# One-hot tables made by two wide VectorE instructions, and gate-table evictions with the token as innermost index

## The chip, the cores and the metric

The kernel runs on one core of a Trainium2 chip. TensorE multiplies matrices, VectorE and ScalarE work elementwise, GpSimd (POOL) does a little elementwise work, and each of them, with SyncE (SP), can issue DMAs. The metric is the time of one execution in microseconds on the device.

## What is computed

Two transformer blocks follow one another on 256 tokens of width 1024. The first mixes tokens by an mLSTM and by differential attention and then applies `peer`, a layer of 16384 one-neuron experts; the second has sparse attention, a convolution and a feed-forward layer. The change lies in `peer`:

```python
def block(xb):                                    # 128 tokens
    q = (xb @ w_query).reshape(TOKEN_BLOCK, P_HEADS, 2, P_HALF)
    s = jnp.einsum('thpk,hpnk->thpn', q, sub_keys).astype(jnp.float32)
    sv, si = lax.top_k(s, P_TOPK)                 # 16 best of 128, for each half
    cand = sv[:, :, 0, :, None] + sv[:, :, 1, None, :]
    cidx = si[:, :, 0, :, None] * N_KEYS + si[:, :, 1, None, :]
    fv, fpos = lax.top_k(cand, P_TOPK)            # (last two axes flattened)
    eidx = jnp.take_along_axis(cidx, fpos, axis=-1)
    g = jax.nn.softmax(fv, axis=-1)
    u = u_tab[eidx]
    act = jax.nn.gelu(jnp.einsum('td,thkd->thk', xb, u), approximate=False)
    return jnp.einsum('thk,thkd->td', (g * act), v_tab[eidx])
```

So each token has 8 heads x 16 = 128 picked experts, each with a gate `g`. An expert's number is (first key) x 128 + (second key).

## The kernel before

The kernel gathers nothing. It computes the activations of all 128 blocks of 128 experts for all 256 tokens, and multiplies them by a gate table that is zero for experts that were not picked. For one block `b`, the unit `U(b)` loads a weight block of `peer_u`, splits it into a high and a low part (`whi`, a ScalarE cast at line 112; `wlo`, a VectorE subtraction at line 120), and `chunk` runs 8 x 3 matmuls of 128x256 (lines 163 to 165). ScalarE applies the gelu (line 793) and writes `act[b]`. Units are converted four to five ahead of their use (`fill`), and loads, of two units each, run in three buffers (`wraw`) on SP's queue.

The gate table is built in the loop at lines 947 to 965, in 32 groups of 8 tokens (`OG`). The 128 partitions are a token's 128 picks. `ib[:, 0]` and `ib[:, 1]` hold the first and the second key of each pick, `gp[:, 0]` and `gp[:, 1]` the gate as a high and a low part, `iob` the numbers 0 to 127 in f16. For each token `onehots` writes with VectorE `o`, a one-hot row of the second key (line 941), and `go`, the one-hot row of the first key times the gate, once for each part (line 943): 24 instructions of 128 elements for a group. TensorE multiplies `o` (stationary) by both parts of `go` (line 958), which gives a 128x128 matrix for the token: 16 matmuls for a group, four tokens to a PSUM bank. ScalarE copies a bank, scaled, to `stg` (line 961), with the tokens `TG` = 16 elements to a row there; after two groups a DMA on ScalarE's queue writes `stg` to the table `gd` in DRAM (line 963). Behind each group stands one unit `U`.

The order is the order of the code on each engine. In a group: `onehots` of the next group, the matmuls and evictions of this one, every second time the DMA, then the unit with its `whi`, `wlo`, matmuls and gelu. `o` and `go` have two buffers, the two PSUM tiles of `side()` and the two of `main()` likewise.

After the loop seven units remain; then the expert loop (lines 1015 to 1023) multiplies each `act` by its part of the table, reread from DRAM as `gt` (line 979), splits the product into `wh` and `wl` (lines 996 and 1001) and accumulates it with `peer_v` into four PSUM banks.

Of the kernel before, what the change touches and what calls it, by code (L numbers as in the profile page):

```python
# [13 lines left out]
F32 = mybir.dt.float32  # L14
F32R = mybir.dt.float32r
BF = mybir.dt.bfloat16
F16 = mybir.dt.float16
# [3 lines left out]
OP = mybir.AluOpType  # L21
# [4 lines left out]
T = 256  # L26
# [9 lines left out]
UKEEP = 7  # L36
TG = 16
OG = 8
GI = 8
LOADS = 9  # L40
SPLITS = 4
GSCALE = 32768.0
# [22 lines left out]
class Kx:  # L65
# [696 lines left out]
    def peer(self):  # L762
        nc, tc, a = self.nc, self.tc, self.a
# [4 lines left out]
        drp = ctx.enter_context(tc.tile_pool(name="pdr", bufs=1, space=DRAM))  # L768
        c1 = ExitStack()
        pz = c1.enter_context(tc.tile_pool(name="pz", bufs=1))  # L770
        gp = pz.tile([128, 2, T], F32, name="gp")
        ib = pz.tile([128, 2, T], F32, name="ib")
        acts = {}
        c2 = ExitStack()
        pk = c2.enter_context(tc.tile_pool(name="pk", bufs=1))
# [20 lines left out]
        with c2:  # L796
# [39 lines left out]
            for hd in range(1, 8):  # L836
# [5 lines left out]
                for i in range(2 if hd > 1 else 0):  # L842
                    p = self.unit("w_query", 2 * hd + i, h)
# [11 lines left out]
            pf_ = c2.enter_context(tc.tile_pool(name="pf", bufs=1))  # L855
# [4 lines left out]
            def finish():  # L860
                g = [pf_.tile([128, 8, 16], F32, name=f"g{tt}") for tt in range(2)]
                pf = [pf_.tile([128, 2, 8, 16], F32, name=f"pf{tt}") for tt in range(2)]
                sxf = [pf_.tile([128, 2, 8, 16], F32, name=f"sxf{tt}") for tt in range(2)]
                for tt in range(2):
                    v = fv[tt]
                    nc.vector.tensor_tensor(g[tt], v, v[:, :, 0:1].to_broadcast([128, 8, 16]), op=OP.subtract)
                    nc.scalar.activation(g[tt], g[tt], AF.Exp)
                for tt in range(2):
                    pi = pft.tile([128, 2, 8, 16], U32, name="pi")
                    nc.vector.tensor_scalar(pi[:, 0], fx[tt], 4, None, op0=OP.logical_shift_right)  # L870
                    nc.vector.tensor_scalar(pi[:, 1], fx[tt], 15, None, op0=OP.bitwise_and)
                    nc.vector.tensor_copy(sxf[tt].rearrange("p s h a -> p h s a"), sx[tt])
                    nc.vector.tensor_copy(pf[tt], pi)
                for tt in range(2):
                    gz = pft.tile([128, 8], F32, name="gz")
                    nc.vector.tensor_reduce(gz, g[tt], axis=AX.X, op=OP.add)
                    nc.vector.reciprocal(gz, gz)
                    nc.vector.tensor_tensor(g[tt], g[tt], gz[:, :, None].to_broadcast([128, 8, 16]), op=OP.mult)
                for _ in range(FW):
                    yield  # L880
                for tt in range(2):
                    p = self.side()
                    for j, src in enumerate((sxf[tt][:, 0], sxf[tt][:, 1], pf[tt][:, 0], pf[tt][:, 1])):
                        nc.tensor.transpose(p[:, j * 128:(j + 1) * 128], src.rearrange("p a b -> p (a b)"),
                                            self.ident)
                    ts = slice(tt * 128, (tt + 1) * 128)
                    p = p.rearrange("p (k s t) -> p k s t", k=2, s=2)
                    nc.scalar.copy(sxT[:, :, ts], p[:, 0])
                    nc.scalar.copy(posT[:, :, ts], p[:, 1])
                p = self.side()  # L890
                for tt in range(2):
                    nc.tensor.transpose(p[:, tt * 128:(tt + 1) * 128], g[tt].rearrange("p a b -> p (a b)"),
                                        self.ident)
                slot = pf_.tile([128, T], F32, name="slot")
                nc.scalar.mul(slot, p[:, :T], GSCALE)
                yield
                acc = self.bank(0)
                last = None
                for a0 in range(0, 16, FA):
                    cur = []  # L900
                    for a in range(a0, a0 + FA):
                        pb = self.side()
                        nc.tensor.matmul(pb, pick[:, a].rearrange("p h w -> p (h w)"),
                                         sxT.rearrange("p s t -> p (s t)"), start=True, stop=True)
                        t = pft.tile([128, 2 * T], BF, name="hit", bufs=2 * FA)
                        nc.vector.scalar_tensor_tensor(t, posT.rearrange("p s t -> p (s t)"), float(a), pb,
                                                       op0=OP.is_equal, op1=OP.mult)
                        cur.append((a, t))
                    yield
                    for a, t in cur:  # L910
                        nc.tensor.matmul(acc, identb, t, start=a == 0, stop=a == 15)
                nc.scalar.copy(ib, acc.rearrange("p (j t) -> p j t", j=2))
                g16 = pf_.tile([128, T], F16, name="g16")
                nc.vector.tensor_copy(g16, slot)
                nc.vector.tensor_copy(gp[:, 0], g16)
                nc.vector.tensor_tensor(gp[:, 1], slot, gp[:, 0], op=OP.subtract)

            self.side_cycle = ("s", "s", "a1", "a2")
            self.tasks.append(finish())
            while self.tasks:  # L920
                self.tick()
                if len(pre) > T // OG + UKEEP:
                    U(pre.popleft())
            while len(pre) > T // OG + UKEEP:
                U(pre.popleft())
            self.side_cycle = ("s",)

        with ExitStack() as c3:
            pg = c3.enter_context(tc.tile_pool(name="pg", bufs=1))
            pgt = c3.enter_context(tc.tile_pool(name="pgt", bufs=2))  # L930
            iob = pg.tile([128, 128], F16, name="iob")
            nc.gpsimd.iota(iob, pattern=[[1, 128]], base=0, channel_multiplier=0,
                           allow_small_or_imprecise_dtypes=True)
            stg = None

            def onehots(og):
                o = pgt.tile([128, OG, 128], F16, name="o")
                go = pgt.tile([128, OG, 2, 128], F16, name="go")
                for i in range(OG):
                    t = slice(og * OG + i, og * OG + i + 1)  # L940
                    nc.vector.tensor_scalar(o[:, i], iob, ib[:, 1, t], None, op0=OP.is_equal)  # L941
                    for j in range(2):
                        nc.vector.tensor_scalar(go[:, i, j], iob, ib[:, 0, t], gp[:, j, t],  # L943
                                                op0=OP.is_equal, op1=OP.mult)
                return o, go

            nxt = onehots(0)
            for og in range(T // OG):
                o2, go = nxt
                if og + 1 < T // OG:  # L950
                    nxt = onehots(og + 1)
                if og % (TG // OG) == 0:
                    stg = pgt.tile([128, 128, TG], F32, name="stg")
                for q in range(OG // 4):
                    p = self.side().rearrange("p (t i) -> p t i", t=4)
                    for i in range(4):
                        for j in range(2):
                            nc.tensor.matmul(p[:, i], o2[:, q * 4 + i], go[:, q * 4 + i, j],  # L958
                                             start=i == 0 and j == 0, stop=j == 1, skip_group_check=True)
                    e0 = (og % (TG // OG)) * OG + q * 4  # L960
                    nc.scalar.mul(stg[:, :, e0:e0 + 4].rearrange("p i t -> p t i"), p, 1.0 / GSCALE)
                if og % (TG // OG) == TG // OG - 1:
                    nc.scalar.dma_start(gd[:, og * OG // TG], stg)
                if len(pre) > UKEEP:
                    U(pre.popleft())
# [3 lines left out]
        with ExitStack() as c4:  # L969
# [5 lines left out]
            def gload(i):  # L975
                if i * GI < NB:
                    gts[i] = gt = pv.tile([128, 8 * (T + 2)], F32, name="gt")[:, :8 * T].rearrange(
                        "p (g e) -> p g e", g=T // TG)
                    (nc.gpsimd if i < 2 else nc.scalar).dma_start(gt, gd[:, :, i * GI:(i + 1) * GI].rearrange("p g i t -> p g (i t)"))

            wts = {}

            def w_mult(b):
                if b >= NB:
                    return
                t = acts[b]
                gv = gts[b // GI][:, :, (b % GI) * TG:(b % GI + 1) * TG]
                tv = t.rearrange("p (g t) -> p g t", t=TG)
                nc.vector.tensor_tensor(tv, tv, gv, op=OP.mult)  # L989
                if b % GI == GI - 1:  # L990
                    gload(b // GI + 2)

# [583 lines left out]
```

## Time and profile before

| | us |
|---|---|
| median of 3 runs | 1547.26 (1546.43 to 1547.27) |
| the profiled execution | 1546.58 |
| span of its trace | 1544.9 |
| TensorE busy in the span | 1427.4 (92%) |
| VectorE busy | 1204.3 (78%) |
| ScalarE busy | 765.9 (50%) |
| GpSimd busy | 240.9 (16%) |

A busy time is the union of an engine's instructions. Matmuls overlap one another, so what a matmul costs is read from the start of one to the start of the next; on VectorE and ScalarE too the next instruction can start a little before the last one's end. The granted clock is TensorE's, as a share of full speed.

### The profile page before, as it was taken

How to read it: one execution, taken by the hardware profiler on the slowest of the kernel's cores; microseconds unless marked ns; L12 is line 12 of the kernel's file. 1: busy time of each engine (PE TensorE's matmuls, PEld its weight loads, DVE VectorE, ACT ScalarE, POOL GpSimd, SP SyncE). 2: the span in 40 equal slices, each digit the busy share in tenths (PEclk: the TensorE clock that was granted, in tenths of full speed). 3: DMA queues.
4: the chain of work that ended last, by engine and by line, in shares of the span. 5: the costliest groups of instructions: out<-in, count | busy, mean ns of one | idle time of the engine just before them, and what ended most of it. 6: DMA issues, size and time to landing. Idle time of an engine off the chain costs nothing.

```text
span 1544.9 us, 28187 instructions
## 1 busy us (share of the span) xinstructions
PE 1427.4 (92%) x11206; PEld 1351.2 (87%) x11208; DVE 1204.3 (78%) x2723; ACT 765.9 (50%) x1225; POOL 240.9 (16%) x143
## 2 busy tenths in 40 slices
PE   3897888979998999999999999999989989999997
PEld 2777777978777779999999999999989979989997
DVE  7887789997999996777777776666689968775554
ACT  3445554434555555544444454454564485554443
POOL 1443253310000000000000000000057740310000
PEclk8898989989999999999999999999999999999999
DMA  9365543434444458888888887677534434435642
GB/s 377 141 239 181 191 150 136 154 122 162 161 167 186 169 206 308 297 307 312 303 308 286 294 285 233 219 244 241 179 114 163 164 109 164 164 138 190 205 165 81
DMA packets 106068, 317.36 MB, mean 205 GB/s; under 512 B 5584, under 2 KB 34640, under 8 KB 103632
## 3 DMA queue, kind: packets, MB, share of 16 engines
q1 hardware_dynamic: 65696, 250.54, 45.8%
q10 hardware_dynamic: 39408, 61.87, 11.4%
q0 software_dynamic: 832, 3.15, 0.6%
q8 instruction: 88, 1.44, 0.4%
q14 instruction: 44, 0.36, 0.1%
HBM read 297.71 MB, written 17.83 MB: 204 GB/s over the span
## 4 chain that ended last, share of the span: by engine, by line
PE 56%; DVE 34%; ACT 4%; DMA 3%; issue 2%; POOL 1%; DVEq 0%; SPq 0%; ACTq 0%; POOLq 0%
PE a L163 10%; PE a L164 10%; PE a L165 10%; PE m L163 8%; PE m L164 8%; PE m L165 8%; DVE go L943 7%; DVE wlo L120 5%; DVE a L1138 3%; DVE o L941 3%; DVE junk L326 2%; DMA mraw<-in_ada_w 1%; ACT whi L112 1%; DMA raw<-in_ada_w 1%; DVE mdt L294 1%
## 5 line engine op out<-in xcount | busy, mean ns | idle before, releaser
L163 PE MATMUL m<-hi,whi 128*128 128x256 f32 x1816 | 526.5, 290 | 9.2 <-DVE cacc L556 6.0
L165 PE MATMUL m<-hi,wlo 128*128 128x256 f32 x1816 | 516.9, 285 | 9.4 <-DVE wlo L120 9.4
L164 PE MATMUL m<-lo,whi 128*128 128x256 f32 x1816 | 517.0, 285 | 0.0
L112 ACT CAST whi<-raw 128x1024 fp32r<-128x1024 f32 x428 | 444.6, 1046 | 50.1 <-DMA raw<-in_peer_v 19.5
L120 DVE TENSOR_TENSOR wlo<-raw,whi 128x1024 fp32r<-128x1024 f32 x350 | 437.7, 1269 | 30.9 <-ACT whi L112 23.0
L163 PEld LDWEIGHTS m<-hi,whi 128*128 128x128 f32 x1816 | 352.1, 194 | 16.1 <-issue 5.4
L165 PEld LDWEIGHTS m<-hi,wlo 128*128 128x128 f32 x1816 | 351.1, 193 | 10.7 <-DVE wlo L120 10.4
L164 PEld LDWEIGHTS m<-lo,whi 128*128 128x128 f32 x1816 | 351.7, 194 | 0.6
L165 PE MATMUL a<-wh,wlo 128*128 128x256 f32 x1024 | 288.2, 281 | 0.0
L164 PE MATMUL a<-wl,whi 128*128 128x256 f32 x1024 | 288.2, 281 | 0.0
L163 PE MATMUL a<-wh,whi 128*128 128x256 f32 x1024 | 287.9, 281 | 0.0
L120 POOL TENSOR_TENSOR wlo<-raw,whi 128x1024 fp32r<-128x1024 f32 x81 | 202.2, 2510 | 223.0 <-ACT whi L112 196.1
L165 PEld LDWEIGHTS a<-wh,wlo 128*128 128x128 f32 x1024 | 192.9, 188 | 0.0
L164 PEld LDWEIGHTS a<-wl,whi 128*128 128x128 f32 x1024 | 192.7, 188 | 0.0
L163 PEld LDWEIGHTS a<-wh,whi 128*128 128x128 f32 x1024 | 192.7, 188 | 0.0
L1001 DVE TENSOR_TENSOR wl<-act,wh 128x256 fp32r<-128x256 f32 x128 | 54.5, 426 | 140.5 <-PE a L164 125.7
L793 ACT ACTIVATE act<-m 128x256 f32<-128x256 f32 x126 | 48.5, 385 | 197.6 <-PE m L165 197.4
L943 DVE TENSOR_SCALAR go<-iob,ib,gp 128x128 f16<-128x128 f16 x512 | 138.8, 319 | 0.0
L996 ACT CAST wh<-act 128x256 fp32r<-128x256 f32 x128 | 51.9, 406 | 141.7 <-DVE act L989 118.8
L326 DVE SCALAR_TENSOR_TENSOR junk<-mraw,silu 128x1024 bf16<-128x1024 f32 x80 | 104.2, 1303 | 6.3 <-DMA mraw<-in_ada_w 6.0
L220 POOL TENSOR_TENSOR act<-act 128x256 f32<-128x256 f32 x7 | 5.6, 800 | 548.7 <-ACT act L211 548.3
L958 PE MATMUL s<-go,o 128*128 128x128 f16 x512 | 74.1, 219 | 18.3 <-DVE go L943 17.5
(438 smaller groups left out, 1962.0 us busy)
## 6 DMA issues: line engine op xcount, KB each, us to landing
raw<-in_peer_u SPq DMA_DIRECT2D x64, 1024.0 KB, 5.8
raw<-in_peer_v SPq DMA_DIRECT2D x64, 1024.0 KB, 5.3
mraw<-in_w_ada ACTq DMA_DIRECT2D x48, 512.0 KB, 5.8
raw<-in_w_ffn_in SPq DMA_DIRECT2D x22, 1024.0 KB, 5.1
gd<-stg ACTq DMA_DIRECT2D x16, 1024.0 KB, 3.9
gt<-gd ACTq DMA_DIRECT2D x14, 1024.0 KB, 8.7
mraw<-in_ada_w SPq DMA_DIRECT2D x24, 512.0 KB, 3.8
raw<-in_w_ffn_out SPq DMA_DIRECT2D x11, 1024.0 KB, 5.0
```

Of the source, the lines that this page charges most:

```text
L112: self.nc.scalar.copy(t, self.raw[k])
L120: eng.tensor_tensor(t, self.raw.pop(k), h.bitcast(F32), op=OP.subtract)
L163: mm(out, w[0], x[0], start=start, stop=False, **kw)
L164: mm(out, w[0], x[1], start=False, stop=False, **kw)
L165: mm(out, w[1], x[0], start=False, stop=stop, **kw)
L326: self.nc.vector.scalar_tensor_tensor(junk, w, 0.5, self.silu_c[i], op0=OP.mult, op1=OP.mult, accum_out=self.mod[i][:, u:u + 1])
L793: nc.scalar.activation(t, p, AF.Gelu)
L941: nc.vector.tensor_scalar(o[:, i], iob, ib[:, 1, t], None, op0=OP.is_equal)
L943: nc.vector.tensor_scalar(go[:, i, j], iob, ib[:, 0, t], gp[:, j, t], op0=OP.is_equal, op1=OP.mult)
L958: nc.tensor.matmul(p[:, i], o2[:, q * 4 + i], go[:, q * 4 + i, j], start=i == 0 and j == 0, stop=j == 1, skip_group_check=True)
L996: nc.scalar.copy(wts[b], acts[b])
L1001: nc.vector.tensor_tensor(wl, acts.pop(b), wts[b].bitcast(F32), op=OP.subtract)
```

## The change

`ib` and `gp` become two parts of one f16 tile `ig`, with the two members of a pair (key 0 and 1, or high and low part) next to each other; `g16` and its copy go. `spread(c)`, a ScalarE copy, writes for a chunk of 16 tokens (`RC`) each of these numbers eight times (`RW`) in a row into `rep`, one chunk ahead of its use. `onehots` is two VectorE instructions of 2048 elements: one compares `iob` with the replicas and makes both one-hot rows of 8 tokens, in `o`; the other multiplies the first key's rows by the two gate parts, in `go`. The matmuls read the second key's rows from `o`. The evictions run over the 128 rows outside and the four tokens inside: they write four neighbouring elements and read PSUM 128 elements apart.

```diff
@@ -36,6 +36,8 @@
 UKEEP = 7
 TG = 16
 OG = 8
+RC = 16
+RW = 8
 GI = 8
 LOADS = 9
 SPLITS = 4
@@ -768,8 +770,8 @@
         drp = ctx.enter_context(tc.tile_pool(name="pdr", bufs=1, space=DRAM))
         c1 = ExitStack()
         pz = c1.enter_context(tc.tile_pool(name="pz", bufs=1))
-        gp = pz.tile([128, 2, T], F32, name="gp")
-        ib = pz.tile([128, 2, T], F32, name="ib")
+        ig = pz.tile([128, 2, T, 2], F16, name="ig")
+        ib, gp = ig[:, 0], ig[:, 1]
         acts = {}
         c2 = ExitStack()
         pk = c2.enter_context(tc.tile_pool(name="pk", bufs=1))
@@ -909,11 +911,9 @@
                     yield
                     for a, t in cur:
                         nc.tensor.matmul(acc, identb, t, start=a == 0, stop=a == 15)
-                nc.scalar.copy(ib, acc.rearrange("p (j t) -> p j t", j=2))
-                g16 = pf_.tile([128, T], F16, name="g16")
-                nc.vector.tensor_copy(g16, slot)
-                nc.vector.tensor_copy(gp[:, 0], g16)
-                nc.vector.tensor_tensor(gp[:, 1], slot, gp[:, 0], op=OP.subtract)
+                nc.scalar.copy(ib.rearrange("p t j -> p j t"), acc.rearrange("p (j t) -> p j t", j=2))
+                nc.vector.tensor_copy(gp[:, :, 0], slot)
+                nc.vector.tensor_tensor(gp[:, :, 1], slot, gp[:, :, 0], op=OP.subtract)
 
             self.side_cycle = ("s", "s", "a1", "a2")
             self.tasks.append(finish())
@@ -933,16 +933,32 @@
                            allow_small_or_imprecise_dtypes=True)
             stg = None
 
+            rep = {}
+
+            def spread(c):
+                if c < T // RC:
+                    sh = [128, 2, RC * 2, RW]
+                    rep[c] = t = pgt.tile(sh, F16, name="rep")
+                    s = ig[:, :, c * RC:(c + 1) * RC].rearrange("p k t j -> p k (t j)")
+                    nc.scalar.copy(t, s[:, :, :, None].to_broadcast(sh))
+
             def onehots(og):
-                o = pgt.tile([128, OG, 128], F16, name="o")
+                c, r = divmod(og * OG, RC)
+                if r == 0:
+                    spread(c + 1)
+                sh = [128, 2 * OG, 128 // RW, RW]
+                i8, g8 = [rep[c][:, k, 2 * r:2 * (r + OG)][:, :, None, :].to_broadcast(sh) for k in range(2)]
+                o = pgt.tile([128, OG, 2, 128], F16, name="o")
                 go = pgt.tile([128, OG, 2, 128], F16, name="go")
-                for i in range(OG):
-                    t = slice(og * OG + i, og * OG + i + 1)
-                    nc.vector.tensor_scalar(o[:, i], iob, ib[:, 1, t], None, op0=OP.is_equal)
-                    for j in range(2):
-                        nc.vector.tensor_scalar(go[:, i, j], iob, ib[:, 0, t], gp[:, j, t],
-                                                op0=OP.is_equal, op1=OP.mult)
-                return o, go
+                v = lambda x: x.rearrange("p t j (a b) -> p (t j) a b", b=RW)
+                io = iob[:, None, :].to_broadcast([128, 2 * OG, 128]).rearrange("p t (a b) -> p t a b", b=RW)
+                nc.vector.tensor_tensor(v(o), i8, io, op=OP.is_equal)
+                nc.vector.tensor_tensor(go.rearrange("p t j (a b) -> p t j a b", b=RW),
+                                        o[:, :, 0:1].to_broadcast([128, OG, 2, 128]).rearrange("p t j (a b) -> p t j a b", b=RW),
+                                        g8.rearrange("p (t j) a b -> p t j a b", j=2), op=OP.mult)
+                return o[:, :, 1], go
+
+            spread(0)
 
             nxt = onehots(0)
             for og in range(T // OG):
@@ -958,7 +974,7 @@
                             nc.tensor.matmul(p[:, i], o2[:, q * 4 + i], go[:, q * 4 + i, j],
                                              start=i == 0 and j == 0, stop=j == 1, skip_group_check=True)
                     e0 = (og % (TG // OG)) * OG + q * 4
-                    nc.scalar.mul(stg[:, :, e0:e0 + 4].rearrange("p i t -> p t i"), p, 1.0 / GSCALE)
+                    nc.scalar.mul(stg[:, :, e0:e0 + 4], p.rearrange("p t i -> p i t"), 1.0 / GSCALE)
                 if og % (TG // OG) == TG // OG - 1:
                     nc.scalar.dma_start(gd[:, og * OG // TG], stg)
                 if len(pre) > UKEEP:
```

On ScalarE's queue around the start of the loop and through its first two groups there stood before (`act` gelu, `stg` eviction, `whi` cast, `gd` write):

```order
L793 ACTIVATE act<-m 128x256
L961 ACTIVATE stg<-s 128x4x128 x2
L112 CAST whi<-raw 128x1024
L793 ACTIVATE act<-m 128x256
L961 ACTIVATE stg<-s 128x4x128 x2
L963 DMA gd<-stg 128x2048
L112 CAST whi<-raw 128x1024
```

and now, on the same queue at the same place (`rep` the replicas):

```order
L795 ACTIVATE act<-m 128x256
L943 COPY rep<-ig 128x512 x2
L977 ACTIVATE stg<-s 128x128x4 x2
L114 CAST whi<-raw 128x1024
L795 ACTIVATE act<-m 128x256
L943 COPY rep<-ig 128x512
L977 ACTIVATE stg<-s 128x128x4 x2
L979 DMA gd<-stg 128x2048
L114 CAST whi<-raw 128x1024
```

Two replica copies stand behind the gelu of the last unit ahead of the loop, and one more ahead of the evictions of every second group.

On VectorE's queue at the same place there stood before (`wlo` the units' low parts, then the narrow one-hots, of which the first pair is shown):

```order
L914 CAST g_3764<-slot 128x256
L915 CAST gp<-g_3764 128x256
L916 TENSOR_TENSOR gp<-slot,gp 128x256
L120 TENSOR_TENSOR wlo<-raw,whi 128x1024 x6
L941 TENSOR_SCALAR o<-iob,ib 128x128
L943 TENSOR_SCALAR go<-iob,ib,gp 128x128 x2
```

and now, on VectorE's queue at the same place:

```order
L915 CAST ig<-slot 128x256
L916 TENSOR_TENSOR ig<-slot,ig 128x256
L122 TENSOR_TENSOR wlo<-raw,whi 128x1024 x6
L955 TENSOR_TENSOR o<-rep,iob 128x2048
L956 TENSOR_TENSOR go<-o,rep 128x2048
L955 TENSOR_TENSOR o<-rep,iob 128x2048
L956 TENSOR_TENSOR go<-o,rep 128x2048
L122 TENSOR_TENSOR wlo<-raw,whi 128x1024
```

Both groups of one-hots that stand ahead of the loop's first `wlo` are now four instructions that read `rep`, where they were 48 that read `ib` and `gp`.

## Rows read from the trace of the kernel before

**Rows 1.** Windows: length, busy of PE, PEld, DVE, ACT, POOL, clock, DMA share, GB/s.
```profile
384.93:570.04 185.11, 167.15 (x1241) 135.28 (x1241) 185.11 (x775) 107.41 (x124) 0.00 (x0) 0.94 0.46 171
570.04:593.00 22.96, 22.96 (x196) 22.96 (x196) 13.85 (x16) 12.50 (x20) 3.61 (x4) 1.00 0.92 320
593.00:1116.00 523.00, 523.00 (x4422) 523.00 (x4421) 369.43 (x546) 250.86 (x372) 0.00 (x0) 1.00 0.78 272
```

**Rows 2.** Waits of TensorE, 384 to 560 us: total us, times, longest.
```profile
PE s L958 <- DVE go L943: 16.7, 98, 0.2
```

**Rows 3.** Timeline of VectorE in the loop: start us, length us.
```profile
563.86 1.23 DVE L120 TENSOR_TENSOR wlo<-raw,whi 128x1024 fp32r<-128x1024 f32 x1
565.00 0.26 DVE L941 TENSOR_SCALAR o<-iob,ib 128x128 f16<-128x128 f16 x1
565.16 0.54 DVE L943 TENSOR_SCALAR go<-iob,ib,gp 128x128 f16<-128x128 f16 x2
565.61 0.26 DVE L941 TENSOR_SCALAR o<-iob,ib 128x128 f16<-128x128 f16 x1
```

**Rows 4.** Timeline of TensorE at the start and the end of the loop.
```profile
382.85 1.05 PE L958 MATMUL s<-go,o 128*128 128x128 f16 x12
...
384.93 0.36 PE L163 MATMUL m<-hi,whi 128*128 128x256 f32 x1
...
562.45 1.17 PE L958 MATMUL s<-go,o 128*128 128x128 f16 x14
...
564.04 0.36 PE L163 MATMUL m<-hi,whi 128*128 128x256 f32 x1
...
566.95 0.85 PE L958 MATMUL s<-go,o 128*128 128x128 f16 x8
...
570.04 0.37 PE L163 MATMUL m<-hi,whi 128*128 128x256 f32 x1
```

**Rows 5.** Timeline of ScalarE in and behind the loop.
```profile
383.05 0.39 ACT L793 ACTIVATE act<-m 128x256 f32<-128x256 f32 x1 [1.51 <-PE m L165]
...
390.03 1.10 ACT L961 ACTIVATE stg<-s 128x512 f32<-128x512 f32 x1 [0.50 <-PE s L958]
...
391.60 1.05 ACT L112 CAST whi<-raw 128x1024 fp32r<-128x1024 f32 x1 [0.47 <-DVE go L943]
...
563.11 2.25 ACT L961 ACTIVATE stg<-s 128x512 f32<-128x512 f32 x2
565.14 1.07 ACT L112 CAST whi<-raw 128x1024 fp32r<-128x1024 f32 x1
567.14 0.38 ACT L793 ACTIVATE act<-m 128x256 f32<-128x256 f32 x1 [0.93 <-PE m L165]
...
586.54 1.04 ACT L112 CAST whi<-raw 128x1024 fp32r<-128x1024 f32 x1
587.49 0.38 ACT L793 ACTIVATE act<-m 128x256 f32<-128x256 f32 x1
```

**Rows 6.** Groups by line and shape: busy us, mean ns | idle before, releasers.
```profile
L961 ACT ACTIVATE stg<-s 128x512 f32<-128x512 f32 x64 | 68.2, 1065 | 42.0 <-PE s L958 40.5
...
L420 ACT COPY hold<-a 128x512 f32<-128x512 f32 x4 | 2.3, 587 | 6.0 <-PE a L165 5.8
...
L110 DVE CAST whi<-raw 128x1024 fp32r<-128x1024 f32 x3 | 2.1, 685 | 0.0
```

**Rows 7.** Timeline of VectorE at the start of the expert loop.
```profile
586.66 0.43 DVE L1001 TENSOR_TENSOR wl<-act,wh 128x256 fp32r<-128x256 f32 x1 [0.52 <-ACT wh L996]
587.01 1.22 DVE L120 TENSOR_TENSOR wlo<-raw,whi 128x1024 fp32r<-128x1024 f32 x1
```

**Rows 8.** Windows in the loop, columns as in rows 1.
```profile
558.00:560.00 2.00, 2.00 (x11) 2.00 (x11) 2.00 (x7) 1.29 (x2) 0.00 (x0) 0.55 0.00 0
560.00:562.00 2.00, 2.00 (x13) 2.00 (x13) 2.00 (x11) 0.84 (x1) 0.00 (x0) 0.59 0.95 393
```

**Rows 9.** The tile `wh`: count, min/median/max ns, first and last start us.
```profile
L163 PE MATMUL a<-wh,whi x1024: 279/281/285, 595.6 to 1126.4; 128*128 128x256 f32 x171
```

## The prediction

> **What bounds the kernel now.** I read the busy time by stretch first. The gate loop (the 32 groups of `peer` at lines 947 to 965) is the one long stretch in which VectorE is busy all the time, 185.11 of 185.11 us, while TensorE's granted clock is 0.94; behind it TensorE is busy without a gap at clock 1.00 until 1116 us [rows 1]. Then the waits of the loop: TensorE's one-hot matmuls (line 958) wait for `go`, 98 times for 16.7 us together, and VectorE waits for nobody [rows 2]. So VectorE sets the period here and TensorE sets it everywhere behind. A period is 570.04 - 384.93 = 185.11 us over 31 starts of a group's `peer_u` unit [rows 4], 5.97 us. VectorE's own rows give the same: one token's three one-hot instructions take 565.61 - 565.00 = 0.61 us, eight tokens 4.88, and one `wlo` 565.00 - 563.86 = 1.14 us; together 6.02 [rows 3].
>
> **What TensorE needs.** In the undisturbed group a unit (24 matmuls) takes 566.95 - 564.04 = 2.91 us, and 14 one-hot matmuls that stand ready take 1.17 us, the last of them 0.22, so 0.073 each and 1.17 for 16 [rows 4]. TensorE's floor is 2.91 + 1.17 = 4.08 us a group. The change leaves its instructions as they are. This floor is the new period if VectorE and ScalarE both stay under it.
>
> **VectorE, part by part.** Removed: 24 narrow instructions a group, 4.88 us. Added: two wide `tensor_tensor` of 2048 f16 elements (`o`, `go`). No row shows a two-input f16 instruction, so I bound one, c, by its neighbours. The f32 `wl` of 256 elements takes 587.01 - 586.66 = 0.35 us to the next instruction and the f32 `wlo` of 1024 takes 1.14 [rows 3, 7]: 1.03 ns an element and 0.09 fixed. At that rate c = 2.20. At two elements a cycle c = 1.14, the price of one `wlo`. Below lies the cast that does 1024 f32 elements in 0.685 [rows 6]; a lower c gains nothing once TensorE is the bound. Above lies the 1x rate with a charge for short runs: an eviction that writes with steps takes 1.065 where one that writes densely takes 0.587 [rows 6], 0.93 ns for each of 512 hops, and 256 runs of 8 elements would add 0.24, so c = 2.44. I take 1.14: the narrow `o` does 128 f16 elements in 565.16 - 565.00 = 0.16 us [rows 3], where the f32 rate would be 0.13 + 0.09 = 0.22, so f16 data already runs faster than one element a cycle here, and the wide operands have runs of 8 with step 1. Then VectorE needs 2 x 1.14 + 1.14 = 3.42 us a group, under 4.08.
>
> The Trainium skill, "VectorE: DVE Perf Modes", section on the perf-mode tier table, gives a two-input instruction on 16-bit SBUF data twice the rate of an f32 one, 1224 ns for 2048 elements. The f32 rate of the trace agrees with its 1x; no run here shows the doubled one. By it the estimated sum is the one below, by the f32 rate it is rival two.
>
> **ScalarE.** The eviction is one instruction as before, now with runs of four tokens written densely and PSUM read in steps. I bound it by the two rows above, 0.587 if the step costs nothing any more and 1.065 if it only moved to the read side. At the high end two in a row take 565.14 - 563.11 = 2.03, `whi` 587.49 - 586.54 = 0.95, the gelu at most 0.39, and the `gd` issue, once in two groups, 391.60 - 390.03 - 1.015 = 0.55 [rows 5]. New is `spread`, 512 elements once in two groups: 0.59 to 1.07 by the same two rows, 0.5 to the next instruction at the lower end. Two groups cost 0.78 + 4.06 + 1.90 + 0.55 + 0.50 = 7.79 us, 3.90 each, so even an eviction that gets no faster hides behind TensorE's 4.08. What is queued behind it: `whi`, then VectorE's `wlo`, and behind that in VectorE's queue the next `o` and `go`. In the dearer group, counted from a unit's start: the gelu starts 567.14 - 564.04 = 3.10 behind it [rows 4, 5] and ends at 3.49, `spread` 3.99, evictions 6.02, issue 6.57, `whi` 7.62, `wlo` 8.79, `go` 11.16, and TensorE wants it at 2 x 4.08 + 2.91 = 11.07. That is 0.1 late at the high end and 0.8 early at the low end, so the period is 4.08 to 4.13 us.
>
> The Trainium skill, "Advanced Engine Details and Errata", section on memory cachelines, speaks against this change: PSUM's lines hold two f32 values and every two consecutive elements should lie together, while SBUF's lines are 16 bytes, which four tokens just fill. The stepped SBUF write is dear in this trace, 1.065 against 0.587; no row shows a stepped PSUM read. By the SBUF half the eviction is estimated at 0.59, by the PSUM half it is rival one.
>
> **The start of the loop.** Now `o` waits for `spread(0)`, which stands in ScalarE's queue behind the gelu of the last unit before the loop, at 383.05 [rows 5]; today VectorE makes the first one-hots beside that unit and TensorE goes on at 382.85 without a gap [rows 4]. After: `spread` ends at about 383.05 + 0.39 + 0.59 = 384.0, `o` and `go` at 386.4, the matmuls at 387.6, where the first unit started at 384.93: 2.7 us lost once. Behind groups with waits TensorE at times runs at half clock: 0.55 and 0.59 in the two stretches from 558 to 562 us [rows 8], which cost 0.9 + 0.8 = 1.7 us. One such stretch may follow this wait; I take half, 0.9.
>
> **At nothing.** `ib` and `gp` in f16 with step 2 lose one narrow instruction, 14 us ahead of the loop, while TensorE is running `peer_u` units already converted. The loads: 171 GB/s at 5.97 us become 250 at 4.08, and the later stretch runs 272 with TensorE full [rows 1]. The last `gd` write goes out some 0.4 us later against the last unit; the first `wl`, made with the gate table, runs at 586.66 [rows 7], while TensorE reads its first `wh` at 595.6 [rows 9], so this has 8 us of cover. If that cover were gone the 0.4 would count. SP and POOL keep their order.
>
> **The sum.** 31 x (5.97 - 4.10) = 58.0, less 2.7 and 0.9, is 54.4 us (4.10 from the 4.08 to 4.13 above). Against the profiled execution's 1546.58 that is 1492.2; the median of the runs is 0.7 higher, so 1492 to 1493. I write 1492. Own range of this case: 1486 (a floor of 3.95, no clock loss) to 1500 (a period of 4.25 and the whole 1.7 lost).
>
> **Rival one: ScalarE becomes the bound.** If the stepped PSUM read charges twice what the stepped write does, 0.587 + 2 x 0.478 = 1.54, two groups cost 7.79 + 4 x 0.48 = 9.7, the period 4.85, and the time is 1546.6 - 31 x 1.12 + 2.7 = 1515. For it: the read steps at every element. Against: PSUM is another memory than the one whose price is known. It decides from an eviction of about 1.2. An eviction between the two gives 1500 to 1515.
>
> **Rival two: the wide instructions run at one element a cycle.** Both at 2.20: period 2 x 2.20 + 1.14 = 5.54, the start costs 4.8, so 1546.6 - 13.3 + 4.8 = 1538. Only `go`, whose pattern has four dimensions: 4.48, TensorE sometimes late, so 4.6, 1508.
>
> **Rival three, slower: one element a cycle and a charge for the short runs.** At c = 2.44 the period is 6.02 and the start costs about 5.3: 1546.6 + 1.6 + 5.3 = 1553. It ends slower as soon as c is over 2.34, since 31 x (4.83 - 2c) is then less than the start's loss. For it: the operands are read in 256 runs of 16 bytes, each replica row again and again. Against: the f16 rate in [rows 3].
>
> **How the numbers follow.** Forecast 0.76, rival one 0.09 (half of it under 1512), rival two 0.08 (half of it the 1508 case), rival three 0.05, under 1486 0.02. The range 1486 to 1512 holds about 0.82. A measurement of this kernel tells about 0.2% from no change. Faster by more: forecast, rivals one and two, 0.93; within: the edge between two and three, 0.02; slower: 0.05.
>
> **What will show it.** `o` and `go` at about 1.2 us each; VectorE with gaps in the loop; starts of units 4.1 us apart; TensorE's waits for `go` gone but for one of some 3.5 us at the loop's start; clock near 1.00 in the loop; evictions at or under 1.07; everything behind the loop moved up unchanged. `o` at 2.2 is rival two, evictions over 1.2 with ScalarE full is rival one. Wrong in a way not listed would be a stretch behind the loop that grows, a wait on `gt` or on `raw` at its start.

## The result and the profile after

The changed kernel takes 1488.06 us (median, 1482.72 to 1488.73), the kernel before 1547.15 in the same comparison: a ratio of 0.961, 95% interval 0.959 to 0.963. The forecast was 1492. The profiled execution after is 1487.78 with a span of 1486.1, 58.8 us less than the span before.

The windows of the kernel after stand at the stages of [rows 1]: the loop, its tail, the expert loop. Columns: length, busy of PE, PEld, DVE, ACT, POOL, clock, DMA share, GB/s.

```profile
389.50:509.30 119.80, 119.80 (x1245) 118.39 (x1245) 111.16 (x93) 82.17 (x139) 0.00 (x0) 0.98 0.79 264
509.30:532.00 22.70, 22.70 (x196) 22.70 (x195) 11.66 (x14) 11.94 (x20) 3.60 (x4) 1.00 0.94 323
532.00:1055.00 523.00, 523.00 (x4421) 523.00 (x4420) 370.18 (x546) 250.48 (x372) 0.00 (x0) 1.00 0.78 272
```

The loop went from 185.11 to about 119.5 us. TensorE is now the engine without a gap, and VectorE has 8.6 us of them, 93 instructions where there were 775. The two stages behind kept their lengths and only moved up: from the last unit of the loop to the first `wh` matmul 25.5 us in both, from the first `wh,whi` matmul of the expert loop to the last 530.9 for 530.8.

TensorE's waits for `go` in the loop were 98 times, 16.7 us [rows 2]. After (total, times, longest):

```profile
PE s L974 <- DVE go L956: 3.6, 1, 3.6
```

TensorE's timeline after, the first wait and three groups (start, length; [ ] is the idle time ahead):

```profile
387.71 1.87 PE L974 MATMUL s<-go,o 128*128 128x128 f16 x16 [3.57 <-DVE go L956]
389.34 0.56 PE L165 MATMUL m<-hi,whi 128*128 128x256 f32 x1
...
394.14 1.07 PE L974 MATMUL s<-go,o 128*128 128x128 f16 x16
...
470.01 1.07 PE L974 MATMUL s<-go,o 128*128 128x128 f16 x16
470.88 0.36 PE L165 MATMUL m<-hi,whi 128*128 128x256 f32 x1
...
473.80 1.07 PE L974 MATMUL s<-go,o 128*128 128x128 f16 x16
```

A period is 473.80 - 470.01 = 3.79 us: 0.87 for the 16 one-hot matmuls (470.88 - 470.01) and 2.92 for the unit. At the start of the loop the same 16 take 389.34 - 387.71 = 1.63, and the unit behind them 394.14 - 389.34 = 4.80.

VectorE's timeline after, in the same group (compare [rows 3]):

```profile
469.72 1.22 DVE L122 TENSOR_TENSOR wlo<-raw,whi 128x1024 fp32r<-128x1024 f32 x1
471.11 1.22 DVE L955 TENSOR_TENSOR o<-rep,iob 128x2048 f16<-128x2048 f16 x1 [0.17 <-PE s L974]
472.37 1.23 DVE L956 TENSOR_TENSOR go<-o,rep 128x2048 f16<-128x2048 f16 x1
473.56 1.23 DVE L122 TENSOR_TENSOR wlo<-raw,whi 128x1024 fp32r<-128x1024 f32 x1
```

A wide instruction of 2048 f16 elements costs what the `wlo` of 1024 f32 elements does: two elements in the time of one. Where nothing waits, VectorE goes 1.26 us from `o` to `go` and 1.14 to 1.19 from each of the other two to the next instruction, so it needs about 3.56 us a group and is the next bound, 0.23 under TensorE.

ScalarE's groups by shape in the loop after (busy us, mean ns | idle before), beside [rows 6]:

```profile
L977 ACT ACTIVATE stg<-s 128x512 f32<-128x512 f32 x64 | 34.9, 597 | 6.1 <-PE s L974 3.4 <-DMA gd<-stg 1.6
L943 ACT COPY rep<-ig 128x512 f16<-128x512 f16 x16 | 9.6, 609 | 0.0
```

The eviction fell from 1.065 to 0.597 us, the price of a dense copy (0.587 in [rows 6]): a PSUM read in steps of 512 bytes costs at most 0.01 us here.

**Where the 58.8 us come from.** I split both profiled executions at five marks; each number is the length after less the length before. From the start to the copy of the keys into `ib`: +1.1. From there to the last gelu ahead of the loop: 0.0. From that gelu to the first unit of the loop: +3.3 (5.16 for 1.88). From the first unit to the last: -65.6 (119.48 for 185.11). From there to the first `wh` matmul: -0.1. From that matmul to the end of the span: +2.5 (951.8 for 949.3); 2.4 of it lie behind the expert loop, with the same instructions and a mean clock of 0.97 where it was 0.98. The sum is -58.8. The +1.1 and +2.5 lie where the change touches nothing, and they are scatter: in the profiled executions of all kernels here the first stretch takes from 360.8 to 370.1 us and the last from 948.1 to 952.1.

### The profile page after: what moved, and what is told of

The parts are those of the page before. It is cut to its first block, busy times and chain, and to the rows that moved or that the text cites. A ratio compares the mean times of both kernels' runs of the same rounds, so it can differ in the third digit from the quotient of the medians.

```text
span 1486.1 us, 27484 instructions
## 1 busy us (share of the span) xinstructions
PE 1385.8 (93%) x11206; PEld 1341.2 (90%) x11208; DVE 1125.2 (76%) x2018; ACT 740.2 (50%) x1241; POOL 243.4 (16%) x143
## 4 chain that ended last, share of the span: by engine, by line
PE 69%; DVE 22%; ACT 4%; DMA 2%; issue 2%; POOL 1%; DVEq 0%; SPq 0%; ACTq 0%; POOLq 0%
PE m L165 11%; PE m L166 11%; PE m L167 11%; PE a L165 10%; PE a L166 10%; PE a L167 10%; DVE a L1154 3%; DVE wlo L122 3%; DVE junk L328 2%; PE s L974 2%; DMA mraw<-in_ada_w 1%; DMA raw<-in_ada_w 1%; DVE mdt L296 1%; DVE lo L303 1%; ACT whi L114 1%
## 5 line engine op out<-in xcount | busy, mean ns | idle before, releaser
L167 PEld LDWEIGHTS m<-hi,wlo 128*128 128x128 f32 x1816 | 347.6, 191 | 8.0 <-DVE wlo L122 8.0
L1005 DVE TENSOR_TENSOR act<-act,gt 128x256 f32<-128x256 f32 x128 | 53.6, 419 | 4.6 <-DMA gt<-gd 4.6
L165 PE MATMUL a<-fh,whi 128*128 128x256 f32 x176 | 49.8, 283 | 0.0
```

Source lines behind the costliest of these rows:

```text
L165: mm(out, w[0], x[0], start=start, stop=False, **kw)
L167: mm(out, w[1], x[0], start=False, stop=stop, **kw)
```

## Experiments

The kernel before took 1547.3, 1548.3 and 1547.4 us in the three groups of runs. The theory: VectorE's wide one-hots alone moved the loop from VectorE's bound to TensorE's, and the start of the loop pays a few us. The rivals: the evictions are part of the gain; the wide instructions are fast only with the replicas' runs of 8.

**The eviction alone, in the kernel before.**

```diff
-                    nc.scalar.mul(stg[:, :, e0:e0 + 4].rearrange("p i t -> p t i"), p, 1.0 / GSCALE)
+                    nc.scalar.mul(stg[:, :, e0:e0 + 4], p.rearrange("p t i -> p i t"), 1.0 / GSCALE)
```

> The kernel before with the new eviction alone. My theory (VectorE's narrow one-hots set the period of 5.97 us): evictions fall to 0.60 us, ScalarE idles more, the period and the time stay, 1546 to 1548. Rival (ScalarE's evictions held the loop through the PSUM tiles): faster by more than 5 us.

Measured 1546.95 us, ratio 1.000 (0.9991 to 1.001). The window of the loop and the group of the eviction:

```profile
384.00:565.00 181.00, 163.77 (x1219) 133.13 (x1218) 181.00 (x755) 78.21 (x122) 0.00 (x0) 0.93 0.46 170
```

```profile
L961 ACT ACTIVATE stg<-s 128x512 f32<-128x512 f32 x61 | 36.5, 599 | 53.0 <-PE s L958 52.4
```

The eviction is 0.47 us cheaper, and ScalarE only waits longer: it is busy for 78.21 of 181 us, where it was 107.41 of 185.11 [rows 1]. VectorE is busy all of the 181 us.

**The old eviction in the changed kernel** (the same two lines, the other way round).

> The changed kernel with the old eviction (token outermost, writes in steps of 64 bytes). My theory (TensorE is the bound at 3.79 us; ScalarE has 0.47 us free in the group with the replica copy and the DMA issue and 1.31 us in the other): evictions back at 1.06 us take 4 x 0.46 = 1.84 us of the 1.78 free in two groups, so the period is 3.79 to 3.9 and the time 0 to 3 us above the changed kernel's. Rival (the eviction carries a good part of the gain): period over 4.1, time over 1498.

Measured 1486.22 us (0.9605, 0.9592 to 0.9618); the changed kernel, run again beside it, 1486.08 (0.9594, 0.9581 to 0.9607). ScalarE's group and its wait for a unit's matmuls in the loop:

```profile
L977 ACT ACTIVATE stg<-s 128x512 f32<-128x512 f32 x64 | 64.6, 1120 | 3.4 <-PE s L974 3.2
```

```profile
ACT act L795 <- PE m L167: 6.9, 16, 2.7
```

ScalarE's pauses ahead of the gelus shrink from 28.8 to 6.9 us, but they don't vanish. VectorE and TensorE in one group of this kernel:

```profile
476.16 1.23 DVE L956 TENSOR_TENSOR go<-o,rep 128x2048 f16<-128x2048 f16 x1
477.30 1.22 DVE L122 TENSOR_TENSOR wlo<-raw,whi 128x1024 fp32r<-128x1024 f32 x1
```

```profile
476.87 1.07 PE L974 MATMUL s<-go,o 128*128 128x128 f16 x16
477.75 0.37 PE L165 MATMUL m<-hi,whi 128*128 128x256 f32 x1
```

The `go` that ends at 477.39 is the one that TensorE takes in the next group, a period of 3.79 later, at 480.66: over 3 us early even here. So the eviction half of the change is worth nothing in this kernel that these runs could tell from scatter, neither alone nor beside the wide one-hots.

What stood on record for the changed kernel's own repeat:

> The changed kernel as it is, beside the others on one chip: 1488 us, a period of 3.79 us a group, one wait of about 3.6 us at the loop's start.

**Runs of two tokens in the eviction.** The four tokens are written as two pairs, with the 128 rows between them.

```diff
-                    nc.scalar.mul(stg[:, :, e0:e0 + 4], p.rearrange("p t i -> p i t"), 1.0 / GSCALE)
+                    nc.scalar.mul(stg[:, :, e0:e0 + 4].rearrange("p i (a b) -> p a i b", b=2), p.rearrange("p (a b) i -> p a i b", b=2), 1.0 / GSCALE)
```

> The changed kernel with the eviction writing runs of two tokens, eight bytes, instead of four. If neighbours in pairs are enough for a dense write: 0.60 us an eviction. If a run must fill 16 bytes: between 0.60 and 1.06, about 0.75 to 0.85 us. The time stays at 1482 to 1488 either way, since ScalarE does not bound the loop.

```profile
L977 ACT ACTIVATE stg<-s 128x512 f32<-128x512 f32 x64 | 36.3, 627 | 4.7 <-PE s L974 3.3 <-DMA gd<-stg 0.2
```

One run, 1485.95 us. An eviction takes 0.627: runs of one f32 word cost 1.07 to 1.12, of two 0.627, of four 0.597. The Trainium skill, "Advanced Engine Details and Errata", section on memory cachelines, gives SBUF lines of 16 bytes, of which two accesses must hit the same line to hide the latency, and PSUM lines of two f32 values, whose neighbours should lie together for the best rate. The SBUF half agrees with these runs: one word to a line is dear, two are nearly as good as four. The PSUM half does not show in them: read one value to a line, an eviction takes 0.597 where a dense copy takes 0.587.

**The wide `o` at one element a cycle.** An operand in f32 takes `o` out of the doubled rate and leaves `go` there.

```diff
-            iob = pg.tile([128, 128], F16, name="iob")
+            iob = pg.tile([128, 128], F32, name="iob")
```

> The changed kernel with iob in f32 instead of f16, so that one operand of the first wide instruction is 32 bits wide and nothing else changes. My theory (the gain rests on two elements a cycle, which needs every operand in 16 bits): o takes 2.2 to 2.3 us instead of 1.22, go stays at 1.22, VectorE needs 2.2 + 1.2 + 1.14 = 4.5 us a group and is the bound again, period 4.5 to 4.6, time about 1487 + 31 x 0.75 + 1 = 1511. Rival (the wide instructions are fast because they are few, whatever their types): o stays at about 1.2 and the time at 1487.

Measured 1510.18 us (0.9756, 0.9739 to 0.9772).

```profile
L955 DVE TENSOR_TENSOR o<-rep,iob 128x2048 f16<-128x2048 f16 x32 | 73.1, 2285 | 4.1 <-ACT rep L943 4.1
```

```profile
472.09 1.07 PE L974 MATMUL s<-go,o 128*128 128x128 f16 x16 [0.65 <-DVE go L956]
...
476.69 1.07 PE L974 MATMUL s<-go,o 128*128 128x128 f16 x16 [0.65 <-DVE go L956]
```

`o` takes 2.285 us, 1.06 more; the period is 4.60, VectorE's own sum (3.56 + 1.06 = 4.62); and TensorE waits 0.65 in each group from the fifth on; the first four live on VectorE's lead. That is the price of rival two's smaller case, forecast there, for `go` in place of `o`, at a period of 4.6 and 1508 us.

**No replicas: runs of one element.**

```diff
-RW = 8
+RW = 1
```

> The changed kernel with one replica in place of eight (RW = 1), so that the wide instructions read each key 128 times with an innermost step of 0. My theory (two elements a cycle need an innermost run of neighbours): both wide instructions run at one element a cycle, 2.2 us each, VectorE needs 5.5 us a group, time about 1487 + 31 x 1.75 + 2 = 1543, a few us under the kernel before. Rival (a repeated element is as good as a run, so the replicas buy nothing): o and go at 1.22, replica copies of 0.2 instead of 0.6 us, time 1486 to 1487.

Measured 1539.99 us (0.9949, 0.993 to 0.9967). Both wide instructions, and two groups of TensorE:

```profile
L956 DVE TENSOR_TENSOR go<-o,rep 128x2048 f16<-128x2048 f16 x31 | 71.1, 2293 | 1.1
L955 DVE TENSOR_TENSOR o<-rep,iob 128x2048 f16<-128x2048 f16 x31 | 70.9, 2288 | 0.0
```

```profile
472.61 1.07 PE L974 MATMUL s<-go,o 128*128 128x128 f16 x16 [1.82 <-DVE go L956]
...
478.28 1.07 PE L974 MATMUL s<-go,o 128*128 128x128 f16 x16 [1.82 <-DVE go L956]
```

Here one operand of each is repeated along the innermost index (its step there is 0), and both instructions run at half the rate, although all data is f16. The period is 5.67 and of 59 us of gain 8 are left. This is rival two in full (forecast 1538), and it shows that the replicas carry nearly the whole gain: two instructions for 24, at the single rate, take only 0.30 us off the period of 5.97.

**Runs of two.** The same line with `RW = 2`: the replicas are a quarter as large, and the runs are 4 bytes.

> The changed kernel with two replicas (RW = 2), runs of two elements, four bytes. If only neighbours in pairs are needed: o and go stay at 1.22 us, the replica copy falls from 0.61 to about 0.3 us, time 1486 to 1487. If every jump between runs costs something, as my slower rival had it (0.93 ns for each of 1024 jumps): o and go at about 2.2 us, period 5.5, time about 1542.

```profile
L956 DVE TENSOR_TENSOR go<-o,rep 128x2048 f16<-128x2048 f16 x32 | 39.2, 1225 | 1.1
L955 DVE TENSOR_TENSOR o<-rep,iob 128x2048 f16<-128x2048 f16 x32 | 39.2, 1224 | 8.2 <-PE s L974 4.5 <-ACT rep L943 3.7
```

Measured 1482.40 us (0.9576, 0.9559 to 0.9592), and again 1484.07 (0.9594, 0.957 to 0.9617). 1024 runs of two cost the same 1.225 as 256 runs of eight, so rival three's charge for each run does not exist on VectorE. `spread` falls from 0.609 to 0.288 us. The intervals overlap those of the changed kernel, so a gain from it can't be told from none.

> Two replicas alone, once more beside the early kernels: between 1482 and 1487 us. My theory gives 0.3 us less than the changed kernel, the rest being its scatter; the rival above gives 1482.

**Half of the one-hot matmuls.** The matmul with the low part of the gate is left out, so the table lacks that part.

```diff
-                        for j in range(2):
+                        for j in range(1):
...
-                                             start=i == 0 and j == 0, stop=j == 1, skip_group_check=True)
+                                             start=i == 0, stop=True, skip_group_check=True)
```

> The changed kernel without the second matmul of each token, so the low part of the gates is left out of the table (go is still made whole). My theory (TensorE is the bound at 3.79 us a group, and VectorE with 1.25 + 1.16 + 1.15 = 3.56 us stands close behind): TensorE's need falls by 8 x 0.057 to 3.34, the period falls only to about 3.57, VectorE has no gaps, time about 1480. Rival (TensorE is not what bounds the loop): the period stays at 3.79.

One run, 1472.24 us. VectorE, then TensorE:

```profile
468.24 1.22 DVE L955 TENSOR_TENSOR o<-rep,iob 128x2048 f16<-128x2048 f16 x1
469.50 1.23 DVE L956 TENSOR_TENSOR go<-o,rep 128x2048 f16<-128x2048 f16 x1
470.64 1.22 DVE L122 TENSOR_TENSOR wlo<-raw,whi 128x1024 fp32r<-128x1024 f32 x1
471.77 1.22 DVE L955 TENSOR_TENSOR o<-rep,iob 128x2048 f16<-128x2048 f16 x1
```

```profile
470.78 0.62 PE L974 MATMUL s<-go,o 128*128 128x128 f16 x8
471.21 0.36 PE L165 MATMUL m<-hi,whi 128*128 128x256 f32 x1
...
474.31 0.62 PE L974 MATMUL s<-go,o 128*128 128x128 f16 x8
```

TensorE would need 2.92 + 0.43 = 3.35, and the period here is 3.53: VectorE runs without a gap again, one `o` to the next 3.53. So TensorE is the bound of the changed kernel, and VectorE stands 0.26 behind it, close to the 0.23 from its rows. Early in the loop the period is TensorE's 3.35:

```profile
398.74 0.62 PE L974 MATMUL s<-go,o 128*128 128x128 f16 x8
...
402.09 0.62 PE L974 MATMUL s<-go,o 128*128 128x128 f16 x8
```

The `go` taken at 398.74 had been ready for 2.2 us. VectorE loses this lead at 0.18 a group, and from about 440 us on its 3.53 is the period. From the first unit of the loop to the last this kernel takes 108.3 us, 11.2 less than in the changed kernel, and the first one-hot matmuls ahead of it take 0.41 for 1.63: 12.4 of the 15.6 us between the two spans. The other 3.2 lie ahead of the `ib` copy (0.5) and behind the first `wh` matmul (2.7), where the kernels do not differ.

**The start of the loop.** Two units are kept back and put behind `spread(0)` and behind the first one-hots, so that TensorE has work while ScalarE and VectorE make these.

```diff
-                if len(pre) > T // OG + UKEEP:
+                if len(pre) > T // OG + UKEEP + 2:
...
-            while len(pre) > T // OG + UKEEP:
+            while len(pre) > T // OG + UKEEP + 2:
...
             spread(0)
-
+            U(pre.popleft())
             nxt = onehots(0)
+            U(pre.popleft())
```

> The changed kernel, but the first replica copy and the first one-hots are issued while two peer_u units are still to run ahead of the loop. My theory (TensorE sets the time from the start of the gate loop to the end of the expert loop, so its 3.57 us wait at the loop's start and the half-clock stretch behind it cost their full length): the wait goes, the first unit of the loop starts 5 to 6 us earlier against the pre-loop units, and the time falls from about 1488 to about 1482. Rival (the wait is made up later, because the gate table or the weights arrive late anyway): the loop starts earlier, but the first matmul of the expert loop does not, and the time stays within 1 us of the changed kernel's.

Measured 1478.71 us (0.9559, 0.9546 to 0.9572), 7.4 under the changed kernel beside it, and again 1477.63 (0.9554, 0.9535 to 0.9572). It beats both kernels. The windows around the start, of the changed kernel and then of this one:

```profile
384.00:388.00 4.00, 0.43 (x6) 0.38 (x5) 2.79 (x3) 1.40 (x3) 0.00 (x0) 0.84 0.36 147
388.00:392.00 4.00, 4.00 (x27) 4.00 (x26) 3.97 (x4) 2.14 (x3) 0.00 (x0) 0.50 0.00 0
392.00:396.00 4.00, 4.00 (x38) 3.96 (x37) 3.44 (x4) 1.66 (x4) 0.00 (x0) 0.81 0.04 8
```

```profile
384.00:388.00 4.00, 4.00 (x44) 3.95 (x43) 3.97 (x4) 2.45 (x5) 0.00 (x0) 1.00 0.73 237
388.00:392.00 4.00, 4.00 (x44) 3.96 (x43) 3.97 (x4) 2.77 (x5) 0.00 (x0) 1.00 0.21 81
392.00:396.00 4.00, 4.00 (x44) 3.95 (x44) 3.93 (x5) 2.57 (x5) 0.00 (x0) 1.00 0.97 314
```

The 3.6 us wait is gone and with it the stretch at half clock behind it. The period stays 3.79. From the `ib` copy to the first `wh` matmul it takes 160.7 us, where the changed kernel took 167.1 and, run again, 166.0: 5.3 to 6.4 of the 7.4 us lie there, about what the wait and the slow clock had cost (2.52 and 2.64, below).

> The kernel whose first one-hots are made two units earlier, once more beside the next two: 1479 us, no wait of TensorE for go.

**Both together**, this start and `RW = 2`.

> The same with two replicas instead of eight. My theory (TensorE is the bound at 3.79 us a group, ScalarE is not, and the first replica copy no longer stands in the way): the copies fall from 0.61 to 0.29 us and the time stays at 1478 to 1480. Rival (ScalarE's shorter queue still buys something, as the 1482 us of two replicas alone against the 1486 of the changed kernel may suggest): 1475 to 1476.

Measured 1482.46 us (0.9575, 0.9551 to 0.96), six runs from 1476.29 to 1486.75: neither figure. Its interval overlaps those of `RW = 2` alone and of the new start alone; three of its six runs lie 4 us and more above every run of the latter, and one lies below them all. In the profiled execution (1484.79) TensorE stops at the start of the expert loop. ScalarE and VectorE there, then TensorE:

```profile
523.04 0.42 DVE L1006 TENSOR_TENSOR act<-act,gt 128x256 f32<-128x256 f32 x1 [10.06 <-DMA gt<-gd]
```

```profile
523.54 0.40 ACT L1013 CAST wh<-act 128x256 fp32r<-128x256 f32 x1 [7.10 <-DVE act L1006]
```

```profile
525.23 0.58 PE L165 MATMUL m<-hi,whi 128*128 128x256 f32 x1 [3.55 <-ACT act L795]
```

The reread table `gt` landed late; the cast `wh` waits for the product with it, stands in ScalarE's queue ahead of the gelu that frees a PSUM tile, and so TensorE stops 3.55 us and goes on at a clock of 0.50 from 525 to 530. The loop itself was as fast as with the new start alone (118.1 us from the first eviction to the last in both). The last write of the table was issued at 502.54 and the reread, which needs it, at 512.04: 9.5 us, 7.8 with the new start alone. The reread's first two transfers then took 12.1 us (median), 9.2 there. Why both were slower, and whether the slower ones of the other five runs stopped there too, is not shown.

## Why the prediction was right, and where its terms were off

**The bound.** Right, and tested from both sides: with `o` at 2.285 the period is VectorE's 4.60, with half of the one-hot matmuls it is VectorE's 3.53, and in the changed kernel TensorE's 3.79, whatever ScalarE's eviction costs.

**TensorE's floor** was the term that was mis-sized, 4.08 to 4.10 for 3.79. I had taken 0.073 us for one of 14 merged matmuls that "stand ready" [rows 4]. They did not stand ready to the end. VectorE's rows ahead of the last one, in the kernel before:

```profile
562.65 0.26 DVE L941 TENSOR_SCALAR o<-iob,ib 128x128 f16<-128x128 f16 x1
562.81 0.54 DVE L943 TENSOR_SCALAR go<-iob,ib,gp 128x128 f16<-128x128 f16 x2
```

That `go` ends at 562.81 + 0.54 = 563.35, and the last of the 14 matmuls starts at 562.45 + 1.17 - 0.22 = 563.40: it waited for it, and the wait is in the 1.17. Back to back one takes (1.07 - 0.22) / 15 = 0.057. The 31 periods therefore gave 31 x 0.31 = 9.6 us more than the sum said.

**c**, the price of a wide instruction: 1.225 long; to the next one 1.25 to 1.26 behind `o` and 1.14 to 1.19 behind `go`, for 1.14. Off by at most 0.12, without effect under TensorE's bound. The Trainium skill, "VectorE: DVE Perf Modes", section on the perf-mode tier table, gives 1224 ns for it in a 16-bit type and 2293 in f32; the trace agrees with the first. Here one operand in f32 (2285) or one repeated along the innermost index (2288 to 2293) is enough for the dearer price.

**ScalarE.** `spread` 0.609 for 0.59; the eviction at its low end. The chain that would have been 0.1 late at the high end was drawn wrongly: `whi` is made one unit further ahead than `wlo`, so `wlo` does not wait for the `whi` just ahead of it in the code but for the one before. With the dear eviction it did wait for that one, 15 times and 8.5 us together from 392 to 509 us, and yet `go` was over 3 us early.

**The start of the loop.** The wait was sized right: 3.57 us of idle, of which 2.52 are lost against the time from gelu to unit before (3.28 less the 0.76 that the first one-hot matmuls take longer), for 2.7. The clock behind it was not: 0.76 and 4.80 - 2.92 = 1.88 make 2.64 us, for 0.9 and over the whole 1.7 that I had allowed. The stretch that I took it from came behind waits of 0.2 us, this one behind 3.57.

**At nothing.** The 8 us of cover at the start of the expert loop were counted to the wrong event. Not the first `wh` matmul decides, but ScalarE's gelu that stands in the queue behind the cast `wh`. After, the product with `gt` comes 524.73 - 508.82 = 15.9 us behind the last unit's start (15.7 before) and TensorE does not stop; with the new start and `RW = 2` it comes at 21.4 and TensorE stops 3.55. Of 5.5 us more, 3.55 were paid, so I estimate the true cover at about 2 us.

**The sum.** 9.6 us more from the period, 0.2 less lost in the wait, 1.7 more lost to the clock, 3.6 lost where nothing changed: 4.5 under the forecast by these terms, 4.4 as measured, 1487.78 for 1492.2. The mechanism was right, but that the total lies this close is in part luck: the floor of 3.79 lies under the 3.95 of the forecast's low end, and the clock and the scatter took back over half of what it gave. The high end of 1500 is rounded up; its own terms give 1498.

**The rivals.** One (ScalarE) falls: neither an eviction of 0.597 nor one of 1.12 bounds the loop. Two did not occur, and was priced rightly: 1510.2 (with `o` in place of `go`) and 1540.0 where it said 1508 and 1538. Three falls: runs of two cost VectorE no more than runs of eight.

## What to carry to other kernels

A mask or one-hot that is made row by row can be made in one wide instruction, if the value that would be repeated along the innermost index is first copied a few times in a row: two in a row are enough for the doubled 16-bit rate, one loses it. When a loop's bound moves from one engine to another, look at the loop's start, where the new first step has no work beside it; two units kept back for that place were worth 5 to 7 us here, the wait and the slow clock behind it. And before a pitch is read from a merged row, check that the last instruction in it did not wait for an input.

## What the runs showed of the hardware

TensorE, after one pause of 3.57 us, ran at half clock for some 5 us (granted clock 0.50 from 388 to 392; unit matmuls 0.213 us apart instead of 0.118 from 389.9 to 393.3), and did not when the pause was filled (1.00 from 384 to 396). ScalarE reads PSUM in steps of 512 bytes at nearly the dense rate (0.597 for 0.587) and is slowed by the stepped write to SBUF (1.07 to 1.12). The write of the table also lands later in the shorter loop; the pages' DMA rows (KB each, median us to landing), before and after:

```profile
gd<-stg ACTq DMA_DIRECT2D x16, 1024.0 KB, 3.9
```

```profile
gd<-stg ACTq DMA_DIRECT2D x16, 1024.0 KB, 8.4
```

The DMA share of the loop rose from 0.46 to 0.79 at the same time. That is not the cause by itself: with half of the one-hot matmuls the share was 0.81 (390 to 495 us), and the writes landed nearly as early as before:

```profile
gd<-stg ACTq DMA_DIRECT2D x16, 1024.0 KB, 4.1
```

What delays them stays open. The first product with `gt` came as far behind the last unit as before (15.9 us, 15.7 before), so this alone cost nothing.
